# Decay matrices of a state-space mixer: the clamped difference of the exponents on ScalarE as a Relu, rather than on VectorE

## The chip, the cores and the metric

The kernel runs on one core of a Trainium2 chip. A core has four compute engines that matter here, each with an instruction queue of its own that it works through in order: TensorE (PE in the rows; matmuls, PEld their weight loads), VectorE (DVE), ScalarE (ACT) and GpSimd (POOL). SyncE (SP) only issues DMAs. Engines wait for each other on semaphores. The metric is the device time of one execution in microseconds (us).

## The reference

Two layers of a hybrid decoder block over 272 tokens (16 learned meta tokens and 256 of the sequence), 2048 wide. Each layer projects the normed input into all its branches at once, mixes tokens in three ways (a pooling mixer, a state-space mixer, sparse attention), and projects back. What matters here is the state-space mixer (SSD): 32 heads in four groups of eight, in chunks of 128 tokens. Inside a chunk it multiplies the products of `C` and `B` by a decay matrix per head:

```python
cs = jnp.cumsum(da, axis=-1)              # da: log decay per token and head, negative
diff = cs[..., :, None] - cs[..., None, :]
mask = jnp.tril(jnp.ones((l, l), dtype=bool))
lm = jnp.where(mask, jnp.exp(jnp.where(mask, diff, 0.0)), 0.0)
cb = jnp.einsum('bclgn,bcsgn->bcgls', cm, bm)
y_diag = jnp.einsum('bcgrls,bcsgrp->bclgrp', cb[:, :, :, None] * lm, xdt)
```

Around it stand a causal convolution and SiLU on `xs`, `B` and `C`, a state that runs from chunk to chunk, a gate `z`, and an RMS norm over each group.

## The kernel before

Everything is float32. The large products (input and output projections) run on TensorE as three products of rounded parts: each weight tile is loaded by DMA (`wr`), ScalarE casts half a tile to its high part (`wh`, L211), VectorE subtracts that from the tile to get the low part (`wl`, L219), and TensorE multiplies (L244 to L246, twelve matmuls for a half of a tile in a block of the input projection). Ten buffers of `wh` let ScalarE cast up to ten halves ahead of TensorE; then the cast waits until TensorE has read an older half.

The projection goes block by block (`q`, `ag`, then for each group `g`: two blocks of `xs`, one of `B` and `C`, two of `z`; then `pv`, `pg`). What follows a block is written as a generator (`post_xs`, `post_BC`, `post_z`, ...). `tick()` lets each live generator go one step; it is called once after each quarter of a block, which is 24 matmuls in the input projection. So the order on every engine is fixed when the program is written out, and in-order queues make one step wait behind another's instructions.

For a group, in program order: `post_xs` convolves (`conv`: L796 on ScalarE, L802 on VectorE, SiLU at L806), transposes on TensorE (`px`, L845 and L847, from the copy `xr`, L826), and scales; `post_xs` also loads `csb` by DMA (L836), the cumulative log decays of the group's eight heads, each row broadcast to all partitions. `post_BC` makes `cbm`, the masked products of `C` and `B`, the states `H`, and then spawns four `decay` generators, each for two heads and one tick after the other. A `decay` writes its two heads of the tile `M` in three steps, a tick apart: the difference of the row's and the column's cumulative sums, clamped at 0 (L935, and L938 for the meta tokens, in layer 0 only); the exponential on ScalarE (L941, L943), with the exponential of `csb` in place (L946); and the product with `cbm` on GpSimd (L948, L950). Column values are in `cs`, one value per partition and head.

`post_z` evaluates the gate (L459, L775), then `ssd_y` lets TensorE multiply by the states (`ph`, L962) and by `M` (`py`, L968; `pym` for the meta tokens), and VectorE reads both (L976, L980), gates (L995, L997), ScalarE squares (L999), GpSimd adds up and splits (L1000 to L1010), TensorE sums over partitions (`pn`, L1014), VectorE scales (L1017), and GpSimd takes the reciprocal root (L272 to L282, the helper `rsqrt_g`). Behind that, in GpSimd's queue, stand products for the next group's `xs` (L860), which ScalarE casts (L864, L865) ahead of the SiLU and the copy `xr` of its second block.

Of the kernel before, what the change touches and what calls it, by code (L numbers as in the profile page):

```python
# [12 lines left out]
AF = mybir.ActivationFunctionType  # L13
OP = mybir.AluOpType
# [88 lines left out]
def hybrid(ctx: ExitStack, tc: tile.TileContext, I, out, dbg=None, layers=2):  # L103
# [15 lines left out]
    V, A, G, TE = nc.vector, nc.scalar, nc.gpsimd, nc.tensor  # L119
# [18 lines left out]
    def bc(ap, shape):  # L138
        return ap.to_broadcast(shape)
# [215 lines left out]
    def layer(L, hs):  # L355
# [108 lines left out]
        cs = wk.tile([P, 3, 32], F32, name="cs", tag="cs")  # L464
# [406 lines left out]
        def post_BC(g, ps):  # L871
# [52 lines left out]
            for c in range(4):  # L924
                spawn(decay(g, c, M, csb, cbm), c)
# [3 lines left out]
        def decay(g, c, M, csb, cbm):  # L929
            hh = slice(2 * c, 2 * c + 2)  # L930
            for h in range(2 * c, 2 * c + 2):
                hg = 8 * g + h
                for b in range(2):
                    sl = slice(16 + b * P, 144 + b * P)
                    V.tensor_scalar(M[:, h, sl], csb[:, h, sl], cs[:, 1 + b, hg:hg + 1], 0.0,  # L935
                                    op0=OP.subtract, op1=OP.min)
                if t0 == 0:
                    V.tensor_scalar(M[0:16, h, 0:16], csb[0:16, h, 0:16], cs[0:16, 0, hg:hg + 1], 0.0,  # L938
                                    op0=OP.subtract, op1=OP.min)
            yield 1  # L940
            A.activation(M[:, hh, 16:], M[:, hh, 16:], AF.Exp)  # L941
            if t0 == 0:
                A.activation(M[0:16, hh, 0:16], M[0:16, hh, 0:16], AF.Exp)  # L943

            for j in range(2):
                A.activation(csb[64 * j:64 * j + 64, 2 * c, 16:], csb[64 * j:64 * j + 64, 2 * c + j, 16:], AF.Exp)  # L946
            yield 1
            G.tensor_tensor(M[:, hh, 16:], M[:, hh, 16:], bc(cbm[:, None, 16:], [P, 2, 256]), op=OP.mult)  # L948
            if t0 == 0:
                G.tensor_tensor(M[0:16, hh, 0:16], M[0:16, hh, 0:16], bc(cbm[0:16, None, 0:16], [16, 2, 16]),  # L950
                                op=OP.mult)
            done.add(f"M{g}_{c}")
# [487 lines left out]
    h = hs  # L1440
    for L in range(layers):
        h = layer(L, h)
# [78 lines left out]
```

## Time and profile before

| | |
|---|---|
| Median of 3 runs | 1574.63 us (1574.49 to 1575.07) |
| Profiled execution, its own time | 1573.18 us |
| Span of its trace, first to last instruction | 1571.4 us |
| TensorE busy | 1533.9 us (98%) |
| VectorE busy | 1204.8 us (77%) |
| ScalarE busy | 884.7 us (56%) |
| GpSimd busy | 417.5 us (27%) |

Busy times are of the same profiled execution; engines work beside each other, so they don't add up. An engine's share over the whole span says little on a stretch of a few microseconds, so the rows below are of single groups. The eight groups (four in each layer) begin their `decay` steps at about 285, 355, 424 and 494 us in layer 0 and 1070, 1138, 1205 and 1273 us in layer 1.

### The profile page before, as it was taken

The page shows a single profiled execution, that of the slowest core. Times are in us where ns is not written, and L with a number is a line of the kernel's source. Part 1 is how long each engine was busy: PE and PEld are TensorE (multiplying, and loading weights), DVE is VectorE, ACT ScalarE, POOL GpSimd, SP SyncE. Part 2 cuts the span into 40 slices and gives each one's busy share as a digit, 9 for nine tenths or more (in the row PEclk, how much of TensorE's full clock was granted, in tenths as well). Part 3 has the DMA queues.
Part 4 walks back from the last instruction along what each step waited for, and adds up shares of the span by engine and source line. Part 5 has one row for each costly group of instructions (what it writes and reads, how often), then busy time and mean ns, then how long its engine had stood idle before and what let it go on. Part 6 is the DMA issues. An engine that isn't in the chain of part 4 may idle for free.

```text
span 1571.4 us, 31133 instructions
## 1 busy us (share of the span) xinstructions
PE 1533.9 (98%) x11788; PEld 1475.4 (94%) x11788; DVE 1204.8 (77%) x2217; ACT 884.7 (56%) x1663; POOL 417.5 (27%) x416
## 2 busy tenths in 40 slices
PE   7999999999999999999998999999999999999997
PEld 7899999999999999999998999999999999988886
DVE  7899777798988776555588998787989888765554
ACT  6455666667667444444455555666676575444542
POOL 3823342233342411000103315322333324200000
PEclk9999999999999999999999999999999999999999
DMA  6545445454554465565536454454545545566652
GB/s 229 209 141 173 145 135 177 148 186 141 189 175 155 135 204 179 191 215 175 174 103 232 152 174 159 148 188 151 194 160 179 181 159 174 183 228 208 209 187 93
DMA packets 78310, 272.44 MB, mean 173 GB/s; under 512 B 8848, under 2 KB 11984, under 8 KB 77136
## 3 DMA queue, kind: packets, MB, share of 16 engines
q1 hardware_dynamic: 78064, 270.39, 51.5%
q8 instruction: 92, 1.51, 0.4%
q14 instruction: 58, 0.48, 0.1%
q10 hardware_dynamic: 96, 0.07, 0.0%
HBM read 266.03 MB, written 4.40 MB: 172 GB/s over the span
## 4 chain that ended last, share of the span: by engine, by line
PE 79%; DVE 10%; POOL 5%; issue 3%; ACT 2%; DMA 1%; SPq 0%; DVEq 0%; ACTq 0%; POOLq 0%
DVE wl L219 4%; PE go L246 4%; PE go L244 4%; PE go L245 4%; PE got L268 4%; PE got L266 4%; PE got L267 4%; PE g0z L244 2%; PE g0z L246 2%; PE g0z L245 2%; PE g1z L244 2%; PE g1z L246 2%; PE g1z L245 2%; PE g0xs L244 2%; PE g1xs L244 2%
## 5 line engine op out<-in xcount | busy, mean ns | idle before, releaser
L219 DVE TENSOR_TENSOR wl<-wr,wh 128x512 fp32r<-128x512 f32 (+1 forms) x952 | 711.2, 773 | 277.1 <-ACT wh L211 74.3
L211 ACT CAST wh<-wr 128x512 fp32r<-128x512 f32 (+1 forms) x952 | 564.8, 615 | 423.3 <-PE go L245 91.7
L244 PE MATMUL g0xs<-u,wh 128*128 128x272 f32 x256 | 74.7, 292 | 0.0
L244 PE MATMUL g1xs<-u,wh 128*128 128x272 f32 x256 | 74.6, 291 | 0.0
L244 PE MATMUL g0z<-u,wh 128*128 128x272 f32 x256 | 74.5, 291 | 0.0
L246 PE MATMUL go<-mixS,wl 128*128 128x272 f32 x256 | 74.1, 290 | 0.0
L246 PE MATMUL g0xs<-u,wl 128*128 128x272 f32 x256 | 74.1, 290 | 0.0
L246 PE MATMUL g0z<-u,wl 128*128 128x272 f32 x256 | 74.1, 290 | 0.0
L246 PE MATMUL g1xs<-u,wl 128*128 128x272 f32 x256 | 74.0, 289 | 0.0
L244 PE MATMUL go<-mixS,wh 128*128 128x272 f32 x256 | 74.0, 289 | 0.0
L245 PE MATMUL g0xs<-u,wh 128*128 128x272 f32 x256 | 73.6, 288 | 0.0
L245 PE MATMUL go<-mixS,wh 128*128 128x272 f32 x256 | 73.6, 287 | 0.0
L245 PE MATMUL g0z<-u,wh 128*128 128x272 f32 x256 | 73.6, 287 | 0.0
L245 PE MATMUL g1xs<-u,wh 128*128 128x272 f32 x256 | 73.6, 287 | 0.0
L244 PE MATMUL g1z<-u,wh 128*128 128x256 f32 x256 | 72.7, 284 | 0.0
L451 POOL TENSOR_TENSOR ropet<-ropet,rope 128x512 f32<-128x512 f32 (+2 forms) x20 | 33.2, 1660 | 147.2 <-PE ptr L483 66.1
L246 PE MATMUL g1z<-u,wl 128*128 128x256 f32 x256 | 71.6, 280 | 0.0
L245 PE MATMUL g1z<-u,wh 128*128 128x256 f32 x256 | 71.6, 280 | 0.0
L948 POOL TENSOR_TENSOR M<-M,cbm 128x512 f32<-128x512 f32 x32 | 45.8, 1431 | 93.3 <-ACT M L941 93.3
L802 DVE SCALAR_TENSOR_TENSOR xs<-xpad,par,xs 128x272 f32<-128x272 f32 x96 | 62.1, 712 | 0.0
L1269 POOL TENSOR_TENSOR acc<-acc,osq 128x544 f32<-128x544 f32 x6 | 8.2, 1366 | 168.8 <-ACT osq L1255 168.8
L266 PE MATMUL got<-wh,mixS 128*128 128x512 f32 x128 | 50.8, 397 | 0.0
(532 smaller groups left out, 5514.1 us busy)
## 6 DMA issues: line engine op xcount, KB each, us to landing
wr<-wi SPq DMA_DIRECT2D x334, 512.0 KB, 3.3
wr<-wo SPq DMA_DIRECT2D x128, 512.0 KB, 3.4
csb<-csd SPq DMA_DIRECT2D x8, 1088.0 KB, 8.6
x<-xT SPq DMA_DIRECT2D x8, 272.0 KB, 5.0
res<-xT SPq DMA_DIRECT2D x4, 544.0 KB, 6.6
h1d<-o SPq DMA_DIRECT2D x4, 544.0 KB, 7.6
wr<-plw SPq DMA_DIRECT2D x8, 256.0 KB, 2.7
hx<-h1d SPq DMA_DIRECT2D x8, 256.0 KB, 3.6
```

What stands on the lines that cost most here:

```text
L211: A.copy(hi, r[:, 2 * h:2 * h + 2])
L219: V.tensor_tensor(lo, r[:, 2 * h:2 * h + 2], his[i].bitcast(F32), op=OP.subtract)
L244: TE.matmul(o, w_h, u[:, 0, k, t1:T], start=first and k == 0, stop=False)
L245: TE.matmul(o, w_h, u[:, 1, k, t1:T], start=False, stop=False)
L246: TE.matmul(o, w_l, u[:, 0, k, t1:T], start=False, stop=last and k == 3)
L266: TE.matmul(o, m_h, hi, start=first, stop=False)
L267: TE.matmul(o, m_h, lo, start=False, stop=False)
L268: TE.matmul(o, m_l, hi, start=False, stop=last)
L451: G.tensor_tensor(t[:, :nch, c0:T], t[:, :nch, c0:T], bc(rope[:, b + 1:b + 2, c0:T], [P, nch, n]), op=OP.mult)
L802: V.scalar_tensor_tensor(dst[:, c], x[:, c, 13 + j:13 + j + T], w[:, j:j + 1], dst[:, c], op0=OP.mult, op1=OP.add)
L948: G.tensor_tensor(M[:, hh, 16:], M[:, hh, 16:], bc(cbm[:, None, 16:], [P, 2, 256]), op=OP.mult)
L1269: G.tensor_tensor(acc[:, :, t0:], acc[:, :, t0:], s[:, :, t0:], op=OP.add)
```

## The change

In `decay`, the difference and the clamp of the two 128x128 blocks of each head go from VectorE (subtract, then minimum with 0, of the column's value) to ScalarE: Relu of the column's value minus the row's, with scale -1 and the column's value as bias. `M` then holds the clamped difference with its sign turned, and the exponential takes scale -1. The 16x16 blocks of the meta tokens stay on VectorE.

```diff
                     sl = slice(16 + b * P, 144 + b * P)
-                    V.tensor_scalar(M[:, h, sl], csb[:, h, sl], cs[:, 1 + b, hg:hg + 1], 0.0,
-                                    op0=OP.subtract, op1=OP.min)
+
+                    A.activation(M[:, h, sl], csb[:, h, sl], AF.Relu, scale=-1.0, bias=cs[:, 1 + b, hg:hg + 1])
                 if t0 == 0:
                     V.tensor_scalar(M[0:16, h, 0:16], csb[0:16, h, 0:16], cs[0:16, 0, hg:hg + 1], 0.0,
                                     op0=OP.subtract, op1=OP.min)
             yield 1
-            A.activation(M[:, hh, 16:], M[:, hh, 16:], AF.Exp)
+            A.activation(M[:, hh, 16:], M[:, hh, 16:], AF.Exp, scale=-1.0)
```

The programs of TensorE, GpSimd and SyncE are the same rows as before. On ScalarE, in the first group of layer 0, from the casts around the first four Relus on (numbers behind a name tell buffers apart; a row with x4 stands for four):

```order
 L211 CAST wh_3792<-wr_3582 128x512
 L211 CAST wh_3810<-wr_3628 128x512
+L936 ACTIVATE M<-csb,cs 128x128 x4
 L211 CAST wh_3833<-wr_3628 128x512
 L211 CAST wh_3851<-wr_3668 128x512
...
 L943 ACTIVATE M<-M 16x2x16
 L946 ACTIVATE csb<-csb 64x256 x2
+L936 ACTIVATE M<-csb,cs 128x128 x4
 L211 CAST wh_3877<-wr_3668 128x512
 L211 CAST wh_3895<-wr_3709 128x512
```

The first four Relus of the group stand between two pairs of casts; the next four behind the exponentials of the first `decay` generator, ahead of two more casts. The third four stand in the same way, and the last four ahead of the table load for the gate:

```order
 L943 ACTIVATE M<-M 16x2x16
 L946 ACTIVATE csb<-csb 64x256 x2
+L936 ACTIVATE M<-csb,cs 128x128 x4
 L775 ACT_TABLE_LOAD
 L775 ACTIVATE gate<-gate 128x544
```

No other row of ScalarE's is added, taken away or moved. On VectorE, at the same place of the program, the splits around them stay where they were:

```order
 L219 TENSOR_TENSOR wl_3812<-wr_3582,wh_3792 128x512
 L927 TENSOR_TENSOR H<-H,pst_3784 128x512
-L935 TENSOR_SCALAR M<-csb,cs 128x128 x2
-L938 TENSOR_SCALAR M<-csb,cs 16x16
-L935 TENSOR_SCALAR M<-csb,cs 128x128 x2
-L938 TENSOR_SCALAR M<-csb,cs 16x16
+L938 TENSOR_SCALAR M<-csb,cs 16x16 x2
 L219 TENSOR_TENSOR wl_3835<-wr_3628,wh_3810 128x512
 L219 TENSOR_TENSOR wl_3853<-wr_3628,wh_3833 128x512
```

Four of 128x128 are gone from this step of the first `decay` generator, and the two of 16x16 are left (none are in layer 1). The split behind them still needs the cast ahead of the first four Relus, and the next split the cast behind them.

## Rows read from the trace of the kernel before

**Rows 1.** The page, part 1: busy us (share of the span) and instructions.

```profile
PE 1533.9 (98%) x11788; PEld 1475.4 (94%) x11788; DVE 1204.8 (77%) x2217; ACT 884.7 (56%) x1663; POOL 417.5 (27%) x416
```

**Rows 2.** TensorE's waits over the whole span: total us, times, longest us.

```profile
PE px L845 <- ACT xr L826: 5.4, 6, 0.9
...
PE pn L1014 <- POOL ysr L1010: 0.3, 1, 0.3
```

**Rows 3.** The chain of waits, 270 to 345 us: start us, us, what.

```profile
312.29 1.10 ACT xs L796 x2
...
320.62 0.45 DVE ysq L1017
...
333.80 0.33 PE px L845
```

**Rows 4.** ScalarE's timeline, layer 0, first group: start us, us, what [idle before].

```profile
283.21 0.62 ACT L211 CAST wh<-wr 128x512 fp32r<-128x512 f32 x1 [0.43 <-PE g0z L245]
...
286.23 0.62 ACT L211 CAST wh<-wr 128x512 fp32r<-128x512 f32 x1 [0.89 <-PE g0z L245]
...
300.57 1.66 ACT L211 CAST wh<-wr 128x512 fp32r<-128x512 f32 x3
```

**Rows 5.** Windows: stretch, us, busy us of PE, PEld, DVE, ACT, POOL; clock, DMA.

```profile
286.23:302.23 16.00, 16.00 (x142) 15.68 (x141) 12.15 (x30) 15.79 (x30) 7.08 (x8) 1.00 0.43 148
```

**Rows 6.** VectorE's timeline, the same group.

```profile
301.22 0.69 DVE L219 TENSOR_TENSOR wl<-wr,wh 128x512 fp32r<-128x512 f32 x1 [2.21 <-ACT wh L211]
...
306.30 0.69 DVE L976 TENSOR_TENSOR yo<-ph,csb 128x512 f32<-128x512 f32 x1 [0.16 <-PE ph L962]
307.34 0.48 DVE L980 SCALAR_TENSOR_TENSOR yg<-xs,par,py 128x256 f32<-128x256 f32 x1 [0.34 <-PE py L968]
...
313.94 0.77 DVE L219 TENSOR_TENSOR wl<-wr,wh 128x512 fp32r<-128x512 f32 x1 [1.65 <-ACT wh L211]
```

**Rows 7.** What reads or writes M, whole span: duration ns min/median/max, starts.

```profile
L935 DVE TENSOR_SCALAR M<-csb,cs x128: 268/278/1395, 284.6 to 1284.0; 128x128 f32<-128x128 f32 x128
...
L948 POOL TENSOR_TENSOR M<-M,cbm x32: 1266/1314/2290, 288.9 to 1287.2; 128x512 f32<-128x512 f32 x32
```

**Rows 8.** ScalarE's groups by shape (busy us, mean ns), then two pieces of its timeline.

```profile
L690 ACT ACTIVATE lg<-lg,nm 128x272 f32<-128x272 f32 x16 | 8.1, 508 | 0.0
L826 ACT COPY xr<-xs 128x128 f32<-128x128 f32 x32 | 8.0, 296 | 0.6
...
L864 ACT CAST xdd<-xr 128x256 fp32r<-128x256 f32 x16 | 6.5, 404 | 14.7 <-POOL xr L860 14.7
...
288.82 0.83 ACT L946 ACTIVATE csb<-csb 64x256 f32<-64x256 f32 x2
...
318.96 0.50 ACT L826 COPY xr<-xs 128x128 f32<-128x128 f32 x2
```

**Rows 9.** VectorE's timeline in layer 1: first group, then the fourth.

```profile
1091.21 0.69 DVE L976 TENSOR_TENSOR yo<-ph,csb 128x512 f32<-128x512 f32 x1 [0.32 <-PE ph L962]
1092.27 0.87 DVE L980 SCALAR_TENSOR_TENSOR yg<-xs,par,py 128x256 f32<-128x256 f32 x2 [0.37 <-PE py L968]
...
1294.05 0.87 DVE L980 SCALAR_TENSOR_TENSOR yg<-xs,par,py 128x256 f32<-128x256 f32 x2 [0.28 <-PE py L968]
```

**Rows 10.** Layer 0: GpSimd's and TensorE's timelines and line L1014, groups one and four.

```profile
301.00 0.24 POOL L950 TENSOR_TENSOR M<-M,cbm 16x32 f32<-16x32 f32 x1
...
315.42 0.86 POOL L1010 TENSOR_TENSOR ysr<-ysq,ysr 128x272 fp32r<-128x272 f32 x1
...
306.19 1.09 PE L968 MATMUL py<-M,xdt 128*64 128x128 f32 x16
...
L1014 PE MATMUL pn<-ysr,ones x2: 289/289/289, 316.7 to 316.8; 128*128 128x272 f32 x2
...
525.29 0.79 POOL L1010 TENSOR_TENSOR ysr<-ysq,ysr 128x272 fp32r<-128x272 f32 x1
...
526.32 0.42 PE L1014 MATMUL pn<-ysr,ones 128*128 128x272 f32 x2
```

## The prediction

> **What bounds the kernel now.** I read the page first: TensorE is busy 1533.9 us of a span of 1571.4 us [rows 1], so only some 37 us of the span are TensorE's idle time, and a change on another engine can win no more than a part of that. It can lose much more: whatever makes TensorE wait is added whole. The second view is the list of TensorE's own waits. Near the change it holds two places [rows 2]: six waits for `px` (the transposes of the next group's `xs`, L845), 5.4 us together, 0.9 us at most each, and one wait of 0.3 us at `pn` (L1014, the sum of squares of a group's output). There is no wait for `M` at L968, the only place where TensorE reads the decay matrices.
>
> The third view is the chain of waits, followed through the first group of layer 0 into the second [rows 3]. Between 312.29 and 333.80 the end is not set by TensorE but by a chain that runs beside it: ScalarE starts the convolution of `xs` (L796), VectorE comes to L1017 at 320.62, GpSimd works through the reciprocal root, ScalarE copies `xr`, and `px` starts at 333.80, late. TensorE hides 20 us of this chain and loses the last 0.9 us. So the question is not which engine is busiest, but whether the change makes this chain start earlier or later.
>
> The fourth view is the timeline of ScalarE ahead of the chain [rows 4]. Up to the cast at 286.23 ScalarE waits for TensorE (0.43 and 0.89 us ahead of the casts shown): it is in time. From there the windows view shows it busy for 15.79 of 16.00 us [rows 5], through table loads, exponentials, a gate and casts, up to the end of three casts in a row at 300.57 + 1.66 = 302.23. VectorE meanwhile waits **for ScalarE** [rows 6]: 2.21 us ahead of the split at 301.22, which needs the first of those three casts. After it VectorE goes straight through its queue, with only 0.16 and 0.34 us of waiting (for TensorE's `ph` and `py`), and then waits 1.65 us for ScalarE again at 313.94. ScalarE and VectorE hand the same delay back and forth.
>
> **The change part by part.** VectorE loses 128 TENSOR_SCALARs of 128x128, 278 ns in the median [rows 7], 16 in each of the eight groups (four groups, two layers). ScalarE gets 128 Relu of 128x128 in the same places of its program, four in each `decay` step. The signs in the exponential cost nothing, since it is the same instruction with another immediate. In the rows of ScalarE's order that front of the text shows, no table load is added.
>
> *What one Relu costs.* The trace has no Relu of this shape. A copy of 128x128 takes 296 ns and one of 128x256 404 ns, so 0.84 ns a column; 272 columns would take 417 ns without operands, and the exponential of 272 columns with a bias column takes 508 ns [rows 8]. The bias column is thus worth 0.09 us and the Relu lasts 296 + 91 = 387 ns. Two copies in a row take 0.50 us rather than 2 x 0.296 = 0.59 [rows 8], so neighbours overlap by 0.09 and one Relu takes ScalarE 0.295 us. From below: 0.205 us, if the bias costs nothing. From above: 0.415 us, as the two exponentials of 64x256 at L946, which do not overlap (0.83 us for two) [rows 8]. I take 0.295, since operands, shape and tiles are nearest to those rows.
>
> *Where they stand.* The first four of a group come behind the cast at 283.21. From its end (283.83) to the cast at 286.23 there are 2.40 us with one cast of 0.62 in them, so 1.78 us are free, and four Relus take 1.27 us: hidden. The other twelve fall between 286.23 and 302.23, where ScalarE has nothing free. They cost 4 x 0.295 = 1.18, 1.18, and 3 x 0.295 + 0.387 = 1.27 us (the last four stand ahead of a table load, which I take to wait for their end): 3.63 us. The three casts move from 300.57 to about 304.2.
>
> *What waits behind that.* VectorE's split at 301.22 moves by 3.63 us, and everything queued behind it with it: `yo`, `yg`, the convolution, L1017. VectorE's saved time (some 0.28 us, sixteen times in each group) becomes a longer wait ahead of that split and is worth nothing. The 0.16 and 0.34 us are won back, since TensorE's `ph` and `py` are then long there: 3.13 us are left. Layer 1 has gaps of 0.32 and 0.37 us there [rows 9]: 2.94 us are left. Its last group has one of 0.28 us: 3.35.
>
> *Where TensorE meets it.* First at `pn`. GpSimd's last instruction ahead of it ends at 315.42 + 0.86 = 316.28 and `pn` starts at 316.7 [rows 10]: a margin of 0.4 us against 3.13, so TensorE waits 2.7 us. At `px` the chain is still 3.13 later and TensorE only 2.7: the wait there grows by the other 0.4, from 0.9 to 1.3. Together the group costs 3.13 us. The fourth group of layer 0 has no `px` behind it, and at `pn` a margin of 526.32 - (525.29 + 0.79) = 0.2 us [rows 10]: 2.9 us. The fourth of layer 1 waits at `pn` already (the 0.3 us in [rows 2]): all 3.35. Since the change leaves TensorE's, GpSimd's and SyncE's programs as they are, and since each group begins with ScalarE again waiting for TensorE, the groups add up:
>
> 3 x 3.13 + 2.9 + 3 x 2.94 + 3.35 = 24.5 us.
>
> What is hidden: the casts themselves. ScalarE casts ten halves of a weight tile ahead, and a half is twelve matmuls, about 1.5 us of TensorE by the spacing of ScalarE's waiting casts; some 15 us of lead bear 3.6 us more. And `M`: GpSimd's last product for the group ends at 301.00 + 0.24 = 301.24 and TensorE reads it from 306.19 [rows 10]; 3.63 us later it is still 1.3 us early.
>
> The profiled execution took 1573.18 us (1571.4 of span, 1.8 around it), the median of the runs is 1574.63, 1.45 more. So 1573.18 + 24.5 = 1597.7 for such an execution and 1574.63 + 24.5 = **1599.1 us** for the median.
>
> *A rule beside it.* By duration a piece goes from 278 ns on VectorE to an estimated 387 ns on ScalarE [rows 7, 8], 0.109 us more. The Trainium skill, ScalarE: Activation LUTs, section Rules for kernel authors, says that relu and min belong on VectorE, which is up to about three times faster per element in bf16. The rows agree on the direction, in fp32 with the fixed part of an instruction far the larger, and by the rule alone, counted as 128 pieces of 0.109 us, the sum would be 14 us and the time 1588.6. I keep the sum by rows, because the price is not the difference of the two engines' times: VectorE's part was beside the chain and ScalarE's is on it.
>
> **The rivals.**
>
> *Faster: VectorE's relief is what counts.* Some of the removed TENSOR_SCALARs took up to 1395 ns instead of 278, and GpSimd's products L948 up to 2290 instead of 1314 [rows 7]: the two disturb each other, and that goes away. If this let VectorE begin its queue at 301.22 earlier, the chain would shorten, the six waits at `px` would vanish, and the time would be 1574.6 - 5.4 = 1569.2. Against it: what VectorE waits for at 301.22 is a cast, not its own queue, and not `M`. It decides only if the three casts at 300.57 come no later than now, that is, if ScalarE had some 3.6 us of hidden waiting between 286.23 and 302.23, where the row shows 0.2. Chance 0.04. The Trainium skill, SBUF — State Buffer, section SBUF: two separate sides, speaks for the disturbance: VectorE and GpSimd share a pair of ports as an exclusive lock, held for the whole instruction. The rows of long TENSOR_SCALARs agree; by that rule alone the gain would be up to those 5.4 us.
>
> *No change.* The delay is swallowed, by the gaps of 0.5 us in VectorE's queue and the margin of 0.4 us at `pn`. That needs less than 0.9 us for twelve Relus, 0.075 us each, or a VectorE that does not really wait for the cast. A plain copy's 0.205 us is far above. Time 1574.6, chance 0.07.
>
> *Slower, but less.* The bias column is hidden: 12 x 0.205 + 0.09 = 2.55 us instead of 3.63, 1.08 less in each of eight groups, so 24.5 - 8.6 = 15.9 us: 1590.5. The same follows if the two engines win back another microsecond of each group in the conversation after 302. Chance 0.13.
>
> *Slower still.* The Relus do not overlap: 12 x 0.415 = 4.98 us, 1.35 more in each group, 24.5 + 10.8 = 35.3 us: 1609.9. From an addition of about 4.9 us on, `M` too comes later than 306.19; that wait lies on the same chain and is not added again. Chance 0.11.
>
> **How the numbers follow.** The forecast has 0.65. Its own range is 1592 to 1605 (a spacing of 0.23 to 0.36 us). The range given goes to the two neighbours, 1585 to 1610: it leaves out faster and no change (0.11) and the outer ends of the two slower rivals (some 0.08). A measurement of this kernel tells about 0.2%, 3.1 us, from no change. Slower by more than that: 0.65 + 0.13 + 0.11 = 0.89; within it 0.07; faster 0.04.
>
> **What would show it.** Right: Relus at L936 of about 0.39 us, 0.3 apart; ScalarE without a gap from the counterpart of the cast at 286.23 to the three casts in a row, now 3.6 us later; VectorE's wait for ScalarE ahead of the split grown well over its 2.21 us, by what was saved and delayed together; and in TensorE's waits a new line of `pn` waiting for GpSimd, eight times, 2.3 to 3.3 us each, with `px` at about 1.3 us or less. TensorE's busy time stays and its idle time grows by 24 us. Wrong would be: `pn` without waits, which says that ScalarE or VectorE had slack that I did not see; waits for `M` at L968 as the main ones, which says that the decay matrices themselves came late; waits for `wh` or `wl`, which says that the lead of the weights ran out; or table loads in front of the Relus.

## The result and the profile after

The changed kernel takes 1601.51 us (median of 4 runs, 1597.74 to 1603.83) against 1574.56 us before on the same chip: the ratio is 1.0165, 95% interval 1.0153 to 1.0177, so 1.65% slower. Its profiled execution took 1602.55 us, with a span of 1600.8. Part 1 of its page, which answers to [rows 1]:

```profile
PE 1545.8 (97%) x11788; PEld 1484.6 (93%) x11788; DVE 1172.9 (73%) x2089; ACT 921.2 (58%) x1791; POOL 413.1 (26%) x416
```

What the tile `M` shows, by instruction (duration in ns, min/median/max), answers to [rows 7]:

```profile
L936 ACT ACTIVATE M<-csb,cs x128: 384/388/404, 286.7 to 1310.2; 128x128 f32<-128x128 f32 x128
...
L948 POOL TENSOR_TENSOR M<-M,cbm x32: 1282/1292/1622, 291.9 to 1315.6; 128x512 f32<-128x512 f32 x32
```

A Relu lasts 388 ns; the prediction had 387. GpSimd's longest product fell from 2290 to 1622 ns, and it bought nothing. That VectorE's TENSOR_SCALARs were what made it long is not shown: in the run below in which no engine does the 128x128 blocks, the longest product takes 1962 ns.

ScalarE's timeline of the first group of layer 0, which answers to [rows 4]. This execution was 3.0 us behind the other when the group began (its `pst` matmuls, L913, start at 283.70 instead of 280.70), so 3.0 is to be taken off when times are compared:

```profile
286.21 0.62 ACT L211 CAST wh<-wr 128x512 fp32r<-128x512 f32 x1 [0.43 <-PE g0z L245]
286.73 1.27 ACT L936 ACTIVATE M<-csb,cs 128x128 f32<-128x128 f32 x4
...
289.23 0.62 ACT L211 CAST wh<-wr 128x512 fp32r<-128x512 f32 x1 [0.71 <-PE g0z L245]
...
292.65 1.28 ACT L936 ACTIVATE M<-csb,cs 128x128 f32<-128x128 f32 x4
...
300.07 1.28 ACT L936 ACTIVATE M<-csb,cs 128x128 f32<-128x128 f32 x4
...
307.17 2.18 ACT L211 CAST wh<-wr 128x512 fp32r<-128x512 f32 x4
```

The first four Relus are gone in the waiting: the cast at 289.23 starts where it did (286.23 + 3.0) and still waits 0.71 us for TensorE. The other twelve are not, and the casts in a row start at 307.17 - 3.0 = 304.17 instead of 300.57, 3.60 us later. There are four of them now, because a fourth fell due in the meantime.

VectorE's timeline of the same group, which answers to [rows 6]:

```profile
303.86 1.29 DVE L219 TENSOR_TENSOR wl<-wr,wh 128x512 fp32r<-128x512 f32 x2 [4.12 <-ACT wh L211]
307.82 0.69 DVE L219 TENSOR_TENSOR wl<-wr,wh 128x512 fp32r<-128x512 f32 x1 [2.67 <-ACT wh L211]
...
312.02 0.73 DVE L997 TENSOR_TENSOR yg<-yg,gate 128x544 f32<-128x544 f32 x1
312.66 0.69 DVE L976 TENSOR_TENSOR yo<-ph,csb 128x512 f32<-128x512 f32 x1
313.26 0.47 DVE L980 SCALAR_TENSOR_TENSOR yg<-xs,par,py 128x256 f32<-128x256 f32 x1
...
319.86 0.75 DVE L219 TENSOR_TENSOR wl<-wr,wh 128x512 fp32r<-128x512 f32 x1 [1.65 <-ACT wh L211]
```

VectorE's saved time became waiting: 4.12 and 2.67 us for ScalarE's casts, where a single wait of 2.21 us stood ahead of the split at 301.22 [rows 6]. The split at 301.22 is now at 304.82 (3.0 taken off), 3.60 later. The two gaps ahead of L976 and L980 are closed. At 319.86 the 1.65 us for ScalarE stand as before: the delay is handed back and forth unchanged.

TensorE's waits over the whole span (total us, times, longest), which answer to [rows 2]:

```profile
PE pn L1014 <- POOL ysr L1010: 13.9, 8, 2.0
...
PE px L845 <- ACT xr L826: 4.0, 3, 1.4
...
PE pn L1014 <- POOL ysr L1008: 1.9, 3, 1.3
```

`pn` is waited for in all eight groups, as forecast. (It has two matmuls, which need two instructions of GpSimd, L1008 and L1010; in three groups the first of them is waited for too, hence the two lines.) `px` is waited for in only three of six places, 1.3 to 1.4 us each; in the other three the wait is gone. What stands in its place is seen in windows around `pn` (the columns are those of [rows 5]: the eighth is TensorE's granted clock), three of the first group and then one of the fourth, layer 0:

```profile
320.00:322.50 2.50, 0.69 (x3) 0.49 (x4) 2.50 (x4) 2.48 (x4) 1.99 (x3) 1.00 0.37 82
322.50:323.70 1.20, 1.20 (x11) 1.20 (x10) 1.20 (x4) 0.18 (x1) 0.00 (x0) 0.95 0.66 266
323.70:327.00 3.30, 3.30 (x17) 3.30 (x16) 3.20 (x6) 2.27 (x6) 0.00 (x0) 0.50 0.18 42
...
542.10:545.60 3.50, 3.50 (x18) 3.50 (x17) 2.37 (x4) 1.17 (x2) 0.83 (x4) 0.52 0.33 122
```

TensorE, after it had been busy only 0.69 of 2.50 us at `pn`, goes on at the full clock for about a microsecond and is then granted half of it (0.50, which is 1.2 instead of 2.4 GHz) for some 3.4 us. What that costs is read from the starts of its matmuls, two ahead of the fall and two behind it:

```profile
322.93 0.29 PE L245 MATMUL g0xs<-u,wh 128*128 128x272 f32 x1
323.05 0.29 PE L246 MATMUL g0xs<-u,wl 128*128 128x272 f32 x1
...
325.32 0.43 PE L246 MATMUL g0xs<-u,wl 128*128 128x272 f32 x1
325.55 0.43 PE L244 MATMUL g0xs<-u,wh 128*128 128x272 f32 x1
```

They start 0.126 us apart at the full clock and 0.227 us apart at half of it (means over 41 and 13 of them), so 3.4 us hold 15 of them rather than 27, and the stretch costs 1.5 us. (The windows count those that began ahead of them, too.) This happened in five of the eight groups, behind last waits at `pn` of 1.7 to 2.0 us; behind the other three, of 1.6 to 1.7 us, it did not.

The sum by groups, from the starts of L913 in the timelines of TensorE (one a group, so that the intervals leave out what differs ahead of the first):

| from group to group, us | before | after | more | clock fell at `pn` |
|---|---|---|---|---|
| layer 0: 1 to 2 | 69.90 | 72.86 | 2.96 | yes |
| 2 to 3 | 69.84 | 72.82 | 2.98 | yes |
| 3 to 4 | 69.85 | 72.71 | 2.86 | no |
| 4 to layer 1's first | 576.24 | 580.86 | 4.62 | yes |
| layer 1: 1 to 2 | 67.45 | 70.10 | 2.65 | no |
| 2 to 3 | 67.44 | 70.41 | 2.97 | yes |
| 3 to 4 | 67.42 | 70.08 | 2.66 | no |
| 4 to the end | 302.56 | 307.26 | 4.70 | yes |

26.4 us together. The remaining 3.0 us of the 29.4 between the two spans lie ahead of the first group, where the programs are the same. This start is not steady: in the seven executions profiled below L913 starts at 281.5 to 284.3 us.

### The profile page after: what moved, and what is told of

It reads as the page before. It is cut to its first block, busy times and chain, and to the rows that moved or that the text cites. A ratio compares the mean times of both kernels' runs of the same rounds, so it can differ in the third digit from the quotient of the medians.

```text
span 1600.8 us, 31092 instructions
## 1 busy us (share of the span) xinstructions
PE 1545.8 (97%) x11788; PEld 1484.6 (93%) x11788; DVE 1172.9 (73%) x2089; ACT 921.2 (58%) x1791; POOL 413.1 (26%) x416
## 4 chain that ended last, share of the span: by engine, by line
PE 79%; DVE 10%; POOL 4%; issue 4%; ACT 2%; DMA 1%; SPq 0%; DVEq 0%; ACTq 0%; POOLq 0%
DVE wl L219 4%; PE go L246 4%; PE go L245 4%; PE go L244 4%; PE got L268 4%; PE got L266 4%; PE got L267 4%; PE g0z L244 2%; PE g0z L246 2%; PE g0z L245 2%; PE g0xs L244 2%; PE g0xs L245 2%; PE g0xs L246 2%; PE g1xs L244 2%; PE g1xs L245 2%
```

## The experiments

The theory on trial: ScalarE has nothing free from the cast at 286.23 on; what counts is how much later the casts in a row come at its end; VectorE passes that on to `pn` and `px`. The rivals: each Relu costs its share wherever it stands; VectorE's relief counts; `M` is late; or it lies in another order of events. Times of before are those of the same chip: 1576.23 us beside the first four Relus, the last four, VectorE relieved and `pn` moved, 1575.14 us beside the other three.

**The first four Relus alone.** The rest is on VectorE as before:

```diff
-                    A.activation(M[:, h, sl], csb[:, h, sl], AF.Relu, scale=-1.0, bias=cs[:, 1 + b, hg:hg + 1])
+                    if c == 0:
+                        A.activation(M[:, h, sl], csb[:, h, sl], AF.Relu, scale=-1.0, bias=cs[:, 1 + b, hg:hg + 1])
+                    else:
+                        V.tensor_scalar(M[:, h, sl], csb[:, h, sl], cs[:, 1 + b, hg:hg + 1], 0.0,
+                                        op0=OP.subtract, op1=OP.min)
...
-            A.activation(M[:, hh, 16:], M[:, hh, 16:], AF.Exp, scale=-1.0)
+            A.activation(M[:, hh, 16:], M[:, hh, 16:], AF.Exp, scale=-1.0 if c == 0 else 1.0)
```

> Only the first of the four decay steps of a group has its four Relus on ScalarE; the other three have the subtraction on VectorE as before. Theory (ScalarE is full only from the cast behind these four on, so what counts is how late the three casts in a row end): the four Relus lie in the 1.78 us that ScalarE waits for TensorE, the casts don't move, 1574.6 us (1573.5 to 1575.6). Rival (each Relu costs its share, wherever it stands): a quarter of 26.9, 6.7 us more, 1581.3. Rival (VectorE's relief counts): a quarter of 5.4 less, 1573.2.

Measured: 1575.35 us, ratio 0.9995 (0.9986 to 1.0004). The intervals between groups are 69.90, 69.85, 69.88 and 67.44, 67.42, 67.42 us, those of before to 0.03. A quarter of the change is free; the share rival, at 1.0043, is out.

**The last four alone.** The same with `c == 3`.

> Only the last of the four decay steps has its Relus on ScalarE, ahead of the gate's table load. Theory: the three casts move by 1.27 us in every group; less the gaps in VectorE's queue (0.50 in layer 0, 0.69 in layer 1, 0.28 in its fourth group) and the margin of 0.2 us of layer 0's fourth group: 3 x 0.77 + 0.57 + 3 x 0.58 + 0.99 = 5.6 us, 1580.2 (1578.5 to 1582). The same number of Relus as in the first run, so the share rival gives 1581.3 for both; only the difference of the two runs tells. Rival (a delay that small is swallowed whole): 1574.6.

Measured: 1580.02 us, ratio 1.0026 (1.0016 to 1.0035), 3.8 us more by the medians and 4.1 by the ratio. The same number of the same instructions, three ticks further down, costs. By intervals it is 0.6 us in each of layer 0's first groups and 0.35 in layer 1's, a little less than the 0.77 and 0.58 expected: the gaps swallow more than was put down for them (below).

**VectorE relieved, ScalarE not loaded.** The exponential reads the row's cumulative sum directly, and the difference and clamp are left out:

```diff
-                    V.tensor_scalar(M[:, h, sl], csb[:, h, sl], cs[:, 1 + b, hg:hg + 1], 0.0,
-                                    op0=OP.subtract, op1=OP.min)
+                    pass
...
-            A.activation(M[:, hh, 16:], M[:, hh, 16:], AF.Exp)
+            A.activation(M[:, hh, 16:], csb[:, hh, 16:], AF.Exp)
```

> Nobody subtracts or clamps: the exponential reads the row's cumulative sum and writes M at once, ScalarE's program is that of before otherwise. So the difference and the clamp of the 128x128 blocks are left out. VectorE is relieved just as in the change, ScalarE has nothing more. Theory: VectorE waits for ScalarE's cast anyway, 1574.6 us (1573.5 to 1575.2). Rival (VectorE's relief and the undisturbed products on GpSimd shorten the chain to px): up to 5.4 us less, 1569.2. Rival (the relief itself does harm by another order of events): over 1577.

Measured: 1575.67 us, ratio 0.9998 (0.9989 to 1.0007), with the six `px` waits of 0.9 us as before. What the change takes off VectorE was worth nothing there.

**The same load, taken off ScalarE elsewhere.** The changed kernel without the exponentials of `csb`, which are left out:

```diff
-            for j in range(2):
-                A.activation(csb[64 * j:64 * j + 64, 2 * c, 16:], csb[64 * j:64 * j + 64, 2 * c + j, 16:], AF.Exp)
```

> The changed kernel without the exponentials of csb in place (L946), which are left out, so that yo is multiplied by the cumulative sum itself. Eight of 64x256 a group, 0.83 us for two, 3.32 us of ScalarE's full stretch, in the place of the 3.63 that twelve Relus added. Theory (ScalarE's time in that stretch, whatever fills it): the three casts come within 0.3 us of where they were before the change, which the gaps in VectorE's queue swallow: 1574.6 us (1573 to 1576.5). Rival (it lies in the Relus or in VectorE's missing subtraction: M late, another order of events): 1597 to 1602.

Measured: 1576.06 us, ratio 1.0007 (0.9998 to 1.0016). All 128 Relus are still there, at 389 ns, and VectorE's 128 subtractions are still gone; with 3.32 us of other work off the same stretch the loss is not to be told from none. So it is ScalarE's time in that stretch, whatever fills it.

**A cheaper Relu.** The changed kernel with the bias left out:

```diff
-                    A.activation(M[:, h, sl], csb[:, h, sl], AF.Relu, scale=-1.0, bias=cs[:, 1 + b, hg:hg + 1])
+                    A.activation(M[:, h, sl], csb[:, h, sl], AF.Relu, scale=-1.0)
```

> The changed kernel with Relu of the turned row alone: the column's value, the bias, is left out of the computation. If the bias column is what makes a Relu last 0.39 rather than 0.30 us, twelve add 2.55 us instead of 3.63: 15.9 us by the same sum as in the prediction, and some 3 more where TensorE's clock falls in the fourth groups: 1590 to 1594. If the time of a Relu does not depend on the bias, or not on the path: 1600 to 1602.

Measured: 1591.72 us, ratio 1.0101 (1.0088 to 1.0115), 16.6 us more instead of 27. The tile `M` there:

```profile
L936 ACT ACTIVATE M<-csb x128: 293/297/315, 286.8 to 1299.8; 128x128 f32<-128x128 f32 x128
```

The bias column costs 388 - 297 = 91 ns of each Relu, and leaving it out takes some 10 us off the loss: 12 x 91 ns in eight groups are 8.7 us, and the clock fell at `pn` in one group instead of five. The Trainium skill, ScalarE: Activation LUTs, section What ACT_TABLE_LOAD costs, gives about 93 ns for each such operand; the trace agrees. In layer 0's fourth group the clock stayed up at `pn`: the second matmul of `pn` and all behind it come 1.8 to 1.9 us later within the group than before, and the interval to layer 1 is 578.30 us, 2.06 more. In layer 1's fourth group it fell: the second matmul of `pn` comes 2.15 us later, the matmuls behind the stretch at half clock 3.7, and the rest of the span is 306.66, 4.10 more. The fall itself is thus worth 1.5 us here, too.

**The first place on TensorE moved away.** The changed kernel with `pn` a tick later and VectorE's next step where it was:

```diff
-            yield PNY
+            yield PNY + 1
             pn = aux("pn")
             for k in range(2):
                 TE.matmul(pn[:, t0:T], ones_r, qs[:, k, t0:], start=k == 0, stop=k == 1)
-            yield 1
+
```

> The changed kernel with the two matmuls pn a tick (24 matmuls) later on TensorE, and VectorE's scaling at L1017 where it was in VectorE's order. Theory: pn is then no longer waited for, and TensorE's clock has no wait of 2 us there behind which it fell to half in five groups; the first three groups of each layer lose as much as now at px (3 x 2.9 + 3 x 2.75 = 17 us), the fourth groups nothing: 1591.6 us (1589.5 to 1593.5), px waits of 3.5 to 4 us, no waits at pn. Rival (the loss is of another place and pn only shows it): 1600 to 1602, with another wait in its stead. Rival (pn is all of it, px follows only because pn was late): 1575 to 1580.

Measured: 1595.2 us, ratio 1.0122 (1.0108 to 1.0136), 19 us more than before and over the expected range. TensorE's waits there:

```profile
PE px L845 <- ACT xr L826: 17.4, 10, 2.0
...
PE ppo L1076 <- DVE pyl L1059: 1.4, 2, 0.8
PE pn L1014 <- POOL ysr L1010: 0.7, 1, 0.7
```

`pn` is no longer waited for except once. The waits are at `px`, not once a group with 3.5 to 4 us but mostly twice, at the transposes of the first block of `xs` with 1.8 to 2.0 us and of the second with 1.6. The first three groups of a layer lose as much as with the change as it is (72.84, 72.63, 72.71 and 70.10, 70.08, 70.09 us from group to group). So in these groups `pn` is only the first place at which the delay is met. The fourth groups were expected to lose nothing and lose 1.0 and 1.8 us: a part of the delay comes through at another place, where the pooling branch's matmuls (`ppo`) wait for VectorE, and in layer 1 at `pn` as well (0.7 us). Still they lose 3.6 and 2.9 us less than with `pn` where it was, some 1.5 us of each because the clock did not fall there; that is most of the 7 us by which the sums of the intervals differ (19.3 here, 26.4 with the change as it is). The clock fell here too, twice, behind waits of 1.9 us at `px`, and not behind one of 2.0.

**The chain by itself, on the kernel before.** L1017 a tick earlier on VectorE, its use where it was:

```diff
                 TE.matmul(pn[:, t0:T], ones_r, qs[:, k, t0:], start=k == 0, stop=k == 1)
-            yield 1
+
...
-            yield PGY
+            yield PGY + 1
```

> The kernel before the change, with VectorE's scaling of pn (L1017) one tick earlier in VectorE's order (ahead of two splits) and its use at L1022 where it was. It tests the chain itself: if L1017 to px is what costs 0.9 us in six groups, 1.2 us earlier takes it away: 1574.6 - 5.4 = 1569.2 us (1568.3 to 1570.5), no waits at px. Rival (px waits are made up elsewhere at once): 1574.6.

Measured: 1572.35 us, ratio 0.9978 (0.9969 to 0.9987): 2.8 us faster than before by the medians and 3.5 by the ratio, less than expected, and the best of all kernels here. The six `px` waits are gone from the list. It wins 0.67 to 0.71 us in each of layer 0's first three groups (intervals of 69.23, 69.14 and 69.14) and 0.57 in layer 1's, 3.7 together rather than the 5.4 of the waits; in layer 1 `pb` behind them (L889, waiting for ScalarE) waits 1.5 us instead of 0.6. The chain from L1017 to `px` is what set the end of these groups before, and it can be shortened by order alone.

## Why the prediction was right, and where it was off

**The price of a Relu** was right to a nanosecond (387 and 388), and so was the overlap: four take 1.27 to 1.28 us.

**The stretch** was right: four hidden, twelve not, the casts 3.60 us later where 3.63 stood. The first-four, last-four and exponential experiments show each half of it.

**What VectorE's gaps give back** was too small. The prediction took the idle time as shown, 0.50 us in layer 0 and 0.69 in layer 1. But neighbours that do not wait also overlap. Ahead of L976 in [rows 6] stood

```profile
305.41 0.72 DVE L997 TENSOR_TENSOR yg<-yg,gate 128x544 f32<-128x544 f32 x1
```

L997 and L976 started 306.30 - 305.41 = 0.89 us apart before and 0.64 after, L976 and L980 1.04 and 0.60. So the two gaps were worth 0.25 + 0.44 = 0.69 us, 0.09 more each, and in layer 1 by the same count 0.87. That gives 3.63 - 0.69 = 2.94 and 3.63 - 0.87 = 2.76 where 3.13 and 2.94 stood, and the groups without a fall of the clock measured 2.86, 2.65 and 2.66.

**Where TensorE meets it**: `pn` first, then `px` with what is left. In the three groups in which the clock stayed up, `px` waits 1.3 to 1.4 us, as forecast. `pn` takes a little less than the forecast 2.7: in layer 0's first three groups L1014's second matmul comes 2.3 to 2.4 us later within its group. (The list of waits shows 1.6 to 2.0 us there, under the 2.3 to 3.3 that the prediction gave for it, since it counts from the end of the matmul before.) In the fourth groups it comes 2.89 and 3.23 us later, where 2.9 and 3.35 stood.

**What was not foreseen** is the clock, and it pays for the other error. Where `px` follows, its cost is nearly hidden: TensorE at half its rate arrives later at a place where it would have waited anyway, so the group loses 2.97 rather than 2.66 us in layer 1, and 2.96 to 2.98 rather than 2.86 in layer 0. In the fourth groups nothing follows, and it is added: behind the stretch at half clock TensorE's matmuls come 4.5 and 4.6 us later within the group than before, and the intervals give 4.62 and 4.70 where 2.9 and 3.35 stood, 3.1 us more together. The sum of the terms was 24.5, the groups measured 26.4. Had the clock stayed up, they would have lost some 22.7 us (an estimate: 3 x 2.86 + 2.89 + 3 x 2.66 + 3.23). So the mechanism was right, but that the time came within 2.4 us of the forecast is in part luck: its own terms were some 1.8 us too large, and the term that it lacked, some 3.7 us, covers that.

One sign of being right did not come: TensorE's busy time was to stay and its idle time to grow by 24 us. Busy time grew from 1533.9 to 1545.8 us and idle time from 37.5 to 55.0, 17.5 more. In the groups in which the clock fell, matmuls at half the rate stand where TensorE would have been idle: it is idle for 1.9 and 1.8 us in layer 0's first two groups, in which the clock fell, and for 3.1 us in the third.

**The rivals.** That VectorE's relief counts is out (third experiment). That the delay is swallowed is out for twelve Relus and true for the first four. That the Relus do not overlap, or that the bias is hidden, is out by the rows. `M` was never waited for: TensorE's list of waits has no line for L968.

Open stays why the clock fell behind five of eight waits at `pn` and not behind the others, three of the five being of the same length (1.69 us) as one that it did not follow; no run here was made to tell what decides it.

## What to carry to other kernels

Before work is moved from a busy engine to one with more idle time, look at who waits for whom in that stretch: here VectorE, at 77%, was waiting for ScalarE, at 56%, and the move loaded the engine that was waited for. A full stretch of 16 us between two waits is where an instruction is paid for, less what gaps further down give back (2.7 to 2.9 of 3.6 us here); the same instruction a few rows earlier was free. And a loss is not over where TensorE stops waiting: behind the waits of 1.6 to 2.0 us at `pn` came, in five of eight groups, a stretch at half the clock, which counts where no later wait hides it.

## What the runs showed of the hardware that was not expected

TensorE's granted clock fell to 0.50 for some 3.4 us behind waits of 1.7 to 2.0 us in an otherwise busy stretch: in four groups 0.3 to 1.4 us after the second matmul of `pn` began, in layer 1's fourth group already in the wait for it. Before the change its waits near there were 0.9 us at most [rows 2], and the windows just behind `pn` showed 1.00; its trace has stretches at half clock, too (from 18, 52, 851 and 1564 us on), but none near a `pn`.

The first 280 us, with the same program, took up to 3.6 us more in one profiled execution than in another (L913 of the first group at 280.70 to 284.32 us). The runs of the kernel before spread by 3.4 and 4.1 us on the two chips of the experiments; whether that is the same thing is not shown, since only profiled executions show where their time goes.
